# Moving the small constant tiles ahead of the large buffers, with one pad tile, in an encoder kernel

## The chip, the cores and the metric

One core of a Trainium2 chip runs the whole program. The metric is device time in microseconds of that core, from one launch; three runs of the kernel before stand behind its median. The core has five engines that work side by side: TensorE (PE, with its weight loads listed apart as PEld), VectorE (DVE), ScalarE (ACT), GpSimd (POOL) and the one that issues DMAs (SP). On-chip memory has 128 partitions; an address here is a byte offset inside a partition, the same in all of them.

## The reference

A two-layer encoder over 512 tokens of width 1024, all in float32. Each layer adds to `x` four blocks, each of the RMS-normed `x`:

```python
x = x + 0.5 * swiglu(rms_norm(x, ffn1_norm[l]), ffn1_w_in[l], ffn1_w_out[l])
h = rms_norm(x, mix_norm[l])
q, k, v, gu, gv, lx, ly, g = jnp.split(h @ w_mix_in[l], MIX_IN_SPLITS, axis=-1)
...
merged = gates[:, :, 0] * y_attn + gates[:, :, 1] * y_gmlp + gates[:, :, 2] * y_lru
x = x + merged @ w_mix_out[l]
x = x + cross_attention(rms_norm(x, xattn_norm[l]), rms_norm(mem, mem_norm[l]), ...)
x = x + 0.5 * swiglu(rms_norm(x, ffn2_norm[l]), ffn2_w_in[l], ffn2_w_out[l])
```

with `swiglu(h) = (silu(h @ w_in[:, :2816]) * (h @ w_in[:, 2816:])) @ w_out`. A last RMS norm gives the output.

## The kernel before

**Arithmetic.** Every float32 matrix product is made of three matmuls in a reduced float32 type: an operand `a` is split into a high part and the remainder, and `mm3` (L354 to L357) adds high x high, high x low and low x high into one PSUM bank. Written `ps<-a,b` in the profile, `a` is the operand that streams through the array and `b` the one that is loaded into it as weights.

**Buffers.** `x` keeps the residual, transposed, as eight tiles of 128 features by 512 tokens; `xh` and `xl` keep the two parts of `x` times the gain of the next norm, in the same layout (2048 bytes per tile and partition). An arena of 14 slots of 8192 bytes, handed out in quarters of 2048, holds everything else that lives for a while. Weights come from memory in chunks of up to 1 MB into two stage buffers (`stage`, L314), and `split` (L329 to L337) turns parts of up to 1024 columns into `whi` on ACT (L336) and `wlo` on DVE (L337), four buffers of 4096 bytes each, up to four parts ahead of their use.

**Products.** In `pair_unit` (the input half of a feed-forward step: 11 times per half pass, 48 matmuls of 512 columns each) and `gate`, `xh`/`xl` stream under 128x128 weights cut from `whi`/`wlo`. In the output half (`ffn`: 8 feature tiles of 33 matmuls) slots stream under the same kind of weights. In `wide_unit` it is the other way round: `whi`/`wlo` stream, 512 columns at a time, under weights cut from `xh`/`xl`; the projections q, gv and gu are made so, and the k/v projection with 256 columns. The memory keys (`xk`) stream slots of 256 columns under `whi`/`wlo`. Each matmul has a weight load of its own, which PE runs beside the matmul before it. Transposes stream the identity in `cst`; the row sums of the norms (`row_scale`, L393) stream slots under `ones_r`, a matrix of ones.

**Order.** The program is written out in full; each engine runs its instructions in the order in which they are written, with the side work (attention, scans, norms) stepped in by `tick` between the products. SP issues all DMAs.

**Addresses.** Memory is given out in the order of the code, each tile rounded up to 32 bytes, from a base of 1152 bytes that the program reserves. As the kernel is built, in bytes:

| buffer | address | modulo 2048 | modulo 512 |
|---|---|---|---|
| x, xh, xl | 1152, 17536, 33920 | 1152 | 128 |
| cst, ones, ones_r | 50304, 52864, 53376 | 1152, 1664, 128 | 128 |
| slots 0 to 13 | 56000 + 8192 i | 704 | 192 |
| stage (2), whi (4), wlo (4) | 170688, 187072, 203456 and up, whole multiples of 4096 apart | 704 | 192 |

Slices of these that a matmul reads start whole multiples of 512 bytes behind the start of the buffer.

Of the kernel before, what the change touches and what calls it, by code (L numbers as in the profile page):

```python
# [6 lines left out]
F32 = mybir.dt.float32  # L7
F32R = mybir.dt.float32r
# [6 lines left out]
P = 128  # L15
D = 1024
KD = D // P
S = 512
# [30 lines left out]
NPC = _c  # L49
ROW = 4 * HD + 512  # L50
NCONST = 128 + 2 * NTT * HD


LAGS = ((2, 2), (1, 2))


def branch_order():
    """Units of the gated sum: gate tiles by number, up projections by pairs of tiles."""
    o = []
    for br, lag in LAGS:  # L60
        for m in range(KD):
            o.append(("gate", br, m))
            if m % 2 == 1 and m >= lag:
                o.append(("up", br, (m - lag) // 2))
        o += [("up", br, c) for c in range((KD - lag) // 2, KD // 2)]
    o += [("gate", 0, m) for m in range(KD)]
    return o + [("up", 0, c) for c in range(KD // 2)]
# [3 lines left out]


def plan():
    """Weight chunks in the order of use: (key, [columns of each part], maker of the [128, columns] array)."""
    out = []

    def add(key, parts, make):
        out.append((key, parts, make))

    def block(name, l, k0, nk, cols, n):  # L80
        def make(w):
            a = w[name][l][k0 * P:(k0 + nk) * P].reshape(nk, P, -1)
            a = np.stack([a[:, :, c:c + n] for c in cols], axis=2)
            return a.transpose(1, 0, 2, 3).reshape(P, -1)
        return make

    def ffn(l, w_in, w_out):
        for b in range(NB):
            for j in range(b * JB, (b + 1) * JB):
                first = l == 0 and j == 0 and w_in == "ffn1_w_in"  # L90
                add((w_in, l, j), [256, 256, 512, 1024] if first else [1024, 1024], block(w_in, l, 0, KD, (j * P, D_FF + j * P), P))
            for m in range(KD):
                add((w_out, l, b, m), [768, 640], block(w_out, l, b * JB, JB, (m * P,), P))

    def pairs(name, l, c0, n, tag):
        for c in range(n):
            add((tag, l, c), [1024, 1024],
                block(name, l, 0, KD, (c0 + 2 * c * P, c0 + (2 * c + 1) * P), P))

    def wide(name, l, c0, tag):  # L100
        for h in range(2):
            add((tag, l, h), [1024, 1024], block(name, l, 4 * h, 4, (c0,), 512))

    def up2(name, l, c):
        u = [block(name, l, 0, 4, ((2 * c + i) * P,), P) for i in range(2)]
        return lambda w: np.concatenate([u[0](w), u[1](w)], axis=1)

    for l in range(L):
        ffn(l, "ffn1_w_in", "ffn1_w_out")
        pairs("w_mix_in", l, LX0, 2, "lx")  # L110
        add(("kv", l), [1024, 1024], block("w_mix_in", l, 0, KD, (K0,), 256))
        wide("w_mix_in", l, Q0, "q")
        pairs("w_mix_in", l, LY0, 2, "ly")
        wide("w_mix_in", l, GV0, "gv")
        wide("w_mix_in", l, GU0, "gu")
        for kind, br, i in BRANCH_ORDER:
            if kind == "gate":
                add(("gate", l, br, i), [1024], block("w_mix_in", l, 0, KD, (G0 + br * D + i * P,), P))
            else:
                add(("up", l, br, i), [1024], up2(("attn_up", "gmlp_up", "lru_up")[br], l, i))  # L120
        pairs("w_mix_out", l, 0, 4, "mo")
        pairs("xattn_wkv", l, 0, 4, "xk")
        pairs("xattn_wq", l, 0, 2, "xq")
        wide("xattn_wkv", l, D, "xv0")
        pairs("xattn_wq", l, 512, 2, "xq")
        wide("xattn_wkv", l, D + 512, "xv1")
        for g in range(2):
            for c in range(2):
                cols = (4 * g * P + 2 * c * P, 4 * g * P + (2 * c + 1) * P)
                add(("wo", l, g, c), [768, 768], block("xattn_wo", l, 0, 6, cols, P))  # L130
            add(("wo2", l, g), [1024], block("xattn_wo", l, 6, 2, tuple((4 * g + i) * P for i in range(4)), P))
        ffn(l, "ffn2_w_in", "ffn2_w_out")
    return out


def pack(w):
    """Lays the inputs out for the chip; moves elements only."""
    f = {n: np.asarray(a) for n, a in w.items()}
    wts = np.concatenate([np.ascontiguousarray(mk(f)).reshape(-1) for _, _, mk in plan()])
    par = np.zeros((P, L, NPC), np.float32)  # L140
# [59 lines left out]


class Arena:
    """Slots of 8 KiB per partition, of either type, given out in quarters; Tile orders the reuse."""

    def __init__(self, pool, n):
        self.pool = pool
# [18 lines left out]
        return best  # L225

    def has(self, *wanted):
        """Whether regions of these (quarters, type) fit together."""
        used = [list(u) for u in self.used]
        kinds = [t[1] for t in self.tiles]  # L230
        for n, dt in wanted:
            b = self.find(n, dt, used, kinds)
            if b is None:
                return False
            used[b[1]][b[2]:b[2] + n] = [True] * n
            kinds[b[1]] = dt
        return True
# [18 lines left out]
def emit(tc, wts, par, rows, ws_t, bd, xt, memt, const, out):  # L256
    nc = tc.nc
    pe, act, dve, pool, sp = nc.tensor, nc.scalar, nc.vector, nc.gpsimd, nc.sync
    chunks = plan()
# [3 lines left out]
    keep = ctx.enter_context(tc.tile_pool(name="keep", bufs=1))  # L263
# [3 lines left out]
    small = ctx.enter_context(tc.tile_pool(name="small", bufs=2))  # L267
    ps_p = ctx.enter_context(tc.tile_pool(name="ps", bufs=8, space=PSUM))

    x = keep.tile([P, KD, S], F32, name="x")  # L270
    xh = keep.tile([P, KD, S], F32R, name="xh")
    xl = keep.tile([P, KD, S], F32R, name="xl")
    cst = keep.tile([P, NCONST], F32, name="cst")
    ones = keep.tile([P, P], F32, name="ones")
    ones_r = keep.tile([P, P], F32R, name="ones_r")
# [2 lines left out]
    mem_row = keep.tile([P, MEM], F32, name="mem_row")  # L278
    pr = [keep.tile([P, NPC], F32, name=f"par{l}") for l in range(L)]
    lam_c = [keep.tile([P, 8], F32, name=f"lam{l}") for l in range(L)]  # L280
    arena = Arena(keep, NSLOT)
    get = arena.get

# [7 lines left out]
    def bank():  # L291
        return ps_p.tile([P, 512], F32, tag="ps", name="ps")

# [1 line left out]
    class Stream:  # L295
        def __init__(self):
            self.parts = []
# [58 lines left out]
        pe.matmul(ps, lhsT=ah, rhs=bl, start=False, stop=False)  # L356
        pe.matmul(ps, lhsT=al, rhs=bh, start=False, stop=stop)  # L357

# [1 line left out]
    tasks = []  # L360
    mark = {}

# [9 lines left out]
        while tasks:  # L372
            tick()

# [1 line left out]
    def rsqrt_small(v, n, tag):  # L376
        b = small.tile([P, n], I32, tag=tag + "b", name="rsb")
        y = small.tile([P, n], F32, tag=tag + "y", name="rsy")
# [7 lines left out]
        return y  # L386

    def row_scale(row, parts, last=None):
        """1 / sqrt(mean + eps) per token of the squares in parts, alike on all partitions."""
        n = row.shape[-1]  # L390
        ps = bank()[:, 0:n]
        for i, a in enumerate(parts):
            pe.matmul(ps, lhsT=ones_r, rhs=a, start=i == 0, stop=last is None and i == len(parts) - 1)  # L393
        if last is not None:
            pe.matmul(ps, lhsT=ones, rhs=last, start=False, stop=True)
        yr, ar = get(1), get(1)
        y, a = yr.f[:, 0:n], ar.f[:, 0:n]
        act.activation(y, ps, AF.Abs_reciprocal_sqrt, scale=1.0 / D, bias=eps_t)
        dve.scalar_tensor_tensor(a, y, -0.5 / D, y, op0=ALU.mult, op1=ALU.mult)
        dve.scalar_tensor_tensor(a, ps, EPS * D, a, op0=ALU.add, op1=ALU.mult)  # L400
        dve.scalar_tensor_tensor(row, a, 1.5, y, op0=ALU.add, op1=ALU.mult)
        yr.free()
        ar.free()

    class Norm:
        """RMSNorm of x by feature tiles: parts of x * gain now, the row scale when all tiles are in."""

        def __init__(self, gain):
            self.gain = gain
# [30 lines left out]
            return row  # L440

    class FinalNorm(Norm):
        """The last RMSNorm, by halves of the tokens, straight to the output."""

        def tile(self, m):
            if m == 0:
# [70 lines left out]
    xhk = [xh[:, k] for k in range(KD)]  # L517
    xlk = [xl[:, k] for k in range(KD)]

# [1 line left out]
    def ffn(l, w_in, w_out, norm, nxt):  # L521
        s_row = None
        for b in range(NB):
# [40 lines left out]
            for g in gs:  # L564
                g.free()

# [1 line left out]
    def mixer(l, norm, nxt):  # L568
        p_ = pr[l]

# [6 lines left out]
        row, gvn = rowr.f[:, 0:4 * HD], gvr.f  # L577
# [135 lines left out]
            gvr.free()  # L713

        def by_token(r, t):
            """Token tile t of [128, (group, token tile, 128)] as [128, group, 128]."""
            return r.f.rearrange("p (g t d) -> p g t d", g=4, t=NTT)[:, :, t]

        def rope(dst, src, t, nh, a_t, b_t):
            """dst = src * A + swapped(src) * B, [128, nh, 64]."""  # L720
            tmp = get(1)
            n = nh * HD
            s3 = src.rearrange("p (h d) -> p h d", h=nh)
# [9 lines left out]
            tmp.free()  # L733

        def head_scale(raw, nh, name):
            """s / sqrt(mean((s raw)^2) + eps) per token and head, laid out [128, head, token tile]."""
            n = nh * HD
            ssq = small.tile([P, nh, NTT], F32, tag=name + "q", name=name + "q")
            for t in range(NTT):
# [165 lines left out]
        lru_task = lru()  # L905
        next(lru_task)

        # input projections
        for c in range(2):
            ps = pair_unit("lx", l, c, xhk, xlk)  # L910
            if c == 0:
# [3 lines left out]
            for i in range(2):  # L915
                t = get(1)
# [25 lines left out]
        for c in range(2):  # L942
            ps = pair_unit("ly", l, c, xhk, xlk)
            for i in range(2):
                t = get(1)
# [17 lines left out]
        for t in range(NTT):  # L963
            act.activation(by_token(u, t), ps[t].rearrange("p (g d) -> p g d", g=4), AF.Gelu_apprx_tanh,
                           scale=scol[:, t:t + 1])
        tasks.append(gmlp())
        tick(3)

        # gates and branch outputs
        def gate(br, m):  # L970
            ps = bank()
            hi, lo = ws.take(("gate", l, br, m))
# [107 lines left out]
        mem_t["h"] = [h3[:, k] for k in range(KD)]  # L1080
        mem_t["l"] = [l3[:, k] for k in range(KD)]

# [1 line left out]
    def xattn(l, norm, nxt):  # L1084
        drain()
        kt_h, kt_l = getr(4), getr(4)
# [145 lines left out]
            r.free()  # L1232

    def lam_prep(l):
        """-8 softplus(-lam): max(-lam, 0) + 2 atanh(e / (2 + e)), e = exp(-|lam|)."""
        lam = pr[l][:, PC["lam"]:PC["lam"] + 8]
        z = [small.tile([P, 8], F32, tag=f"lz{i}", name=f"lz{i}") for i in range(5)]
        dve.tensor_scalar(z[0], lam, -1.0, None, op0=ALU.mult)
# [72 lines left out]
```

## Time and profile before

| | |
|---|---|
| median of three runs | 2709.33 us (2707.06 to 2711.34) |
| profiled execution | span 2707.8 us, 30194 instructions; no other time of its own is given |
| PE busy | 2666.5 us, 98% |
| PEld / DVE / ACT / POOL busy | 81% / 51% / 43% / 15% |
| DMA | 254.31 MB, 94 GB/s on the mean |

A span runs from the first to the last instruction. A busy share is the time in which an engine has at least one instruction under way; matmuls overlap one another, so the time from one start to the next, not the duration of one, tells the pace. PEclk is the granted clock of TensorE in tenths, of which the full one is 2.4 GHz and the lower level 1.2 GHz.

### The profile page before, as it was taken

What the parts mean: (1) busy time and instruction counts of PE and PEld (TensorE: products, weight loads), DVE (VectorE), ACT (ScalarE), POOL (GpSimd) and SP (SyncE); (2) the same over time, 40 slices, a digit from 0 to 9 for tenths busy, and PEclk for the clock granted to TensorE, in tenths of its full rate; (3) what the DMA queues carried; (4) which work ended last, traced back from release to release, by engine and by line L of the source; (5) the groups of instructions that cost most, each with busy time, mean ns of one, the idle gap of its engine ahead of it and who ended that gap; (6) DMA issues with size and microseconds to landing.
All of it is one profiled execution on the core that took longest, in us unless ns stands there. A gap on an engine that the chain in (4) does not pass through costs nothing.

```text
span 2707.8 us, 30194 instructions
## 1 busy us (share of the span) xinstructions
PE 2666.5 (98%) x12213; PEld 2183.8 (81%) x12213; DVE 1387.2 (51%) x1965; ACT 1161.7 (43%) x1655; POOL 401.1 (15%) x301
## 2 busy tenths in 40 slices
PE   8999999999999999999999999989999999999998
PEld 6888888788878888888888888878888888888886
DVE  5433457766655554334443344577675664533333
ACT  5322336866634442222332223478575343422223
POOL 3101115100121021001111011240000300210111
PEclk9999999999999999999999999999999999999999
DMA  5232231222233222232322322321222232322222
GB/s 178 79 114 94 84 114 71 78 71 78 86 109 109 90 97 97 83 109 84 108 97 74 134 94 75 116 78 62 78 78 94 94 125 78 109 84 95 107 76 74
DMA packets 50123, 254.31 MB, mean 94 GB/s; under 512 B 5440, under 2 KB 11072, under 8 KB 31808
## 3 DMA queue, kind: packets, MB, share of 16 engines
q1 hardware_dynamic: 49984, 252.39, 26.4%
q8 instruction: 95, 1.56, 0.2%
q14 instruction: 44, 0.36, 0.0%
HBM read 250.27 MB, written 2.10 MB: 93 GB/s over the span
## 4 chain that ended last, share of the span: by engine, by line
PE 91%; DVE 4%; ACT 2%; POOL 1%; issue 1%; DMA 0%; SPq 0%; DVEq 0%; POOLq 0%; ACTq 0%
PE ps L356 29%; PE ps L355 29%; PE ps L357 29%; PE ps L858 1%; PE ps L829 1%; PE ps L846 1%; POOL slot L1011 1%; DVE wlo L337 1%; DVE slot L484 1%; DVE slot L1007 0%; ACT slot L483 0%; DMA x<-in_xt 0%; DVE rsy L385 0%; ACT whi L336 0%; POOL nacc L427 0%
## 5 line engine op out<-in xcount | busy, mean ns | idle before, releaser
L336 ACT CAST whi<-stage 128x1024 fp32r<-128x1024 f32 (+2 forms) x506 | 490.9, 971 | 1075.0 <-PE ps L356 939.7
L337 DVE TENSOR_TENSOR wlo<-stage,whi 128x1024 fp32r<-128x1024 f32 (+2 forms) x506 | 588.8, 1164 | 485.6 <-ACT whi L336 483.5
L355 PE MATMUL ps<-xh,whi 128*128 128x512 f32 x2048 | 811.7, 397 | 1.7 <-ACT xh L417 1.7
L356 PE MATMUL ps<-xl,whi 128*128 128x512 f32 x2048 | 808.3, 395 | 0.8 <-DVE xl L418 0.7
L357 PE MATMUL ps<-xh,wlo 128*128 128x512 f32 x2048 | 808.1, 395 | 0.0
L355 PE MATMUL ps<-slot,whi 128*128 128x512 f32 (+1 forms) x1291 | 488.0, 378 | 2.6 <-ACT slot L483 2.6
L356 PE MATMUL ps<-slot,whi 128*128 128x512 f32 (+1 forms) x1291 | 487.0, 377 | 1.1 <-DVE slot L484 1.1
L357 PE MATMUL ps<-slot,wlo 128*128 128x512 f32 (+1 forms) x1291 | 486.4, 377 | 0.0
L355 PEld LDWEIGHTS ps<-xh,whi 128*128 128x128 f32 x2048 | 383.7, 187 | 96.5 <-ACT xh L417 3.3
L356 PEld LDWEIGHTS ps<-xl,whi 128*128 128x128 f32 x2048 | 383.7, 187 | 95.8 <-DVE xl L418 2.4
L357 PEld LDWEIGHTS ps<-xh,wlo 128*128 128x128 f32 x2048 | 383.6, 187 | 93.6
L533 POOL TENSOR_TENSOR slot<-slot,srow 128x512 f32<-128x512 f32 x88 | 148.7, 1689 | 928.6 <-ACT slot L532 928.6
L355 PEld LDWEIGHTS ps<-slot,whi 128*128 128x128 f32 x1291 | 242.9, 188 | 48.8 <-ACT slot L483 3.5
L356 PEld LDWEIGHTS ps<-slot,whi 128*128 128x128 f32 x1291 | 243.0, 188 | 46.8 <-DVE slot L484 2.0
L357 PEld LDWEIGHTS ps<-slot,wlo 128*128 128x128 f32 x1291 | 242.9, 188 | 44.5
L483 ACT CAST slot<-slot 128x512 fp32r<-128x512 f32 (+2 forms) x149 | 89.5, 608 | 280.2 <-DVE slot L534 216.0
L427 POOL TENSOR_TENSOR nacc<-nacc,slot 128x512 f32<-128x512 f32 x62 | 97.2, 1567 | 570.7 <-ACT slot L426 299.5
L531 DVE TENSOR_TENSOR slot<-ps,srow 128x512 f32<-128x512 f32 x88 | 60.8, 691 | 229.1 <-PE ps L357 229.0
L484 DVE TENSOR_TENSOR slot<-slot,slot 128x512 fp32r<-128x512 f32 (+2 forms) x149 | 103.4, 701 | 91.1 <-ACT slot L483 90.8
L534 DVE TENSOR_TENSOR slot<-slot,ps 128x512 f32<-128x512 f32 x88 | 60.5, 687 | 111.7 <-POOL slot L533 111.7
L484 DVE TENSOR_TENSOR slot<-ps,slot 128x512 fp32r<-128x512 f32 (+1 forms) x144 | 92.5, 655 | 40.4 <-ACT slot L483 39.3
L483 ACT CAST slot<-ps 128x512 fp32r<-128x512 f32 (+1 forms) x144 | 77.3, 564 | 58.7 <-PE ps L357 55.4
(192 smaller groups left out, 2268.6 us busy)
## 6 DMA issues: line engine op xcount, KB each, us to landing
stage<-in_wts SPq DMA_DIRECT2D x141, 1024.0 KB, 4.8
stage<-in_wts SPq DMA_DIRECT2D x64, 704.0 KB, 4.0
stage<-in_wts SPq DMA_DIRECT2D x77, 512.0 KB, 3.2
stage<-in_wts SPq DMA_DIRECT2D x8, 768.0 KB, 4.5
slot<-in_memt SPq DMA_DIRECT2D x6, 512.0 KB, 3.3
slot<-in_bd SPq DMA_DIRECT2D x4, 512.0 KB, 5.9
out<-slot SPq DMA_DIRECT2D x8, 256.0 KB, 2.6
x<-in_xt SPq DMA_DIRECT2D x1, 1024.0 KB, 9.2
```

Source lines behind the costliest of these rows:

```text
L336: act.copy(hi[:, 0:n], t)
L337: dve.tensor_tensor(lo[:, 0:n], t, hi[:, 0:n].bitcast(F32), op=ALU.subtract)
L355: pe.matmul(ps, lhsT=ah, rhs=bh, start=start, stop=False)
L356: pe.matmul(ps, lhsT=ah, rhs=bl, start=False, stop=False)
L357: pe.matmul(ps, lhsT=al, rhs=bh, start=False, stop=stop)
L427: pool.tensor_tensor(self.acc, self.acc, sq.f, op=ALU.add)
L483: act.copy(hi, src)
L484: dve.tensor_tensor(lo, src, hi.bitcast(F32), op=ALU.subtract)
L531: dve.tensor_tensor(t.f, psa, s_row, op=ALU.mult)
L533: pool.tensor_tensor(t.f, t.f, s_row, op=ALU.mult)
L534: dve.tensor_tensor(t.f, t.f, psb, op=ALU.mult)
L829: pe.matmul(ps, lhsT=qt[e].r[:, c0:c0 + P], rhs=kk.r[:, k0:k0 + 512], start=part == 0, stop=part == 1)
```

## The change

The three large tiles `x`, `xh` and `xl` are made behind the small ones instead of ahead of them, and a tile of 336 floats (1344 bytes) that nothing reads or writes is put between. The other lines of the diff take comments and docstrings away.

```diff
+PAD = 336
...
-    x = keep.tile([P, KD, S], F32, name="x")
-    xh = keep.tile([P, KD, S], F32R, name="xh")
-    xl = keep.tile([P, KD, S], F32R, name="xl")
     cst = keep.tile([P, NCONST], F32, name="cst")
     ones = keep.tile([P, P], F32, name="ones")
     ones_r = keep.tile([P, P], F32R, name="ones_r")
...
     pr = [keep.tile([P, NPC], F32, name=f"par{l}") for l in range(L)]
     lam_c = [keep.tile([P, 8], F32, name=f"lam{l}") for l in range(L)]
+    keep.tile([P, PAD], F32, name="pad")
+    x = keep.tile([P, KD, S], F32, name="x")
+    xh = keep.tile([P, KD, S], F32R, name="xh")
+    xl = keep.tile([P, KD, S], F32R, name="xl")
     arena = Arena(keep, NSLOT)
```

By the sizes in the code (NCONST is 640, NPC 120) `cst` then starts at 1152, `ones` at 3712, `ones_r` at 4224, the pad at 6848, `x` at 8192, `xh` at 24576, `xl` at 40960, slot 0 at 57344, the stage buffers at 172032, `whi` at 188416 and `wlo` at 204800. From `x` on, all of these are multiples of 2048.

## Rows read from the trace of the kernel before

**Rows 1.** The page: span, then busy us (share) xinstructions, then PEclk by slices.
```profile
span 2707.8 us, 30194 instructions
...
PE 2666.5 (98%) x12213; PEld 2183.8 (81%) x12213; DVE 1387.2 (51%) x1965; ACT 1161.7 (43%) x1655; POOL 401.1 (15%) x301
...
PEclk9999999999999999999999999999999999999999
```

**Rows 2.** The page: the chain that ended last, shares by engine.
```profile
PE 91%; DVE 4%; ACT 2%; POOL 1%; issue 1%; DMA 0%; SPq 0%; DVEq 0%; POOLq 0%; ACTq 0%
```

**Rows 3.** The list of waits, all engines: us in total, times, longest us.
```profile
ACT whi L336 <- PE ps L356: 939.7, 336, 4.8
...
PE ps L800 <- DVE slot L807: 14.3, 3, 8.2
...
ACT whi L336 <- DMA stage<-in_wts: 8.9, 4, 3.7
```

**Rows 4.** Timeline of PE, 1112 to 1296 us: start, duration, line, op; three rows.
```profile
1112.63 0.39 PE L355 MATMUL ps<-slot,whi 128*128 128x512 f32 x1
...
1172.49 0.39 PE L355 MATMUL ps<-xh,whi 128*128 128x512 f32 x1
...
1295.69 0.39 PE L355 MATMUL ps<-slot,whi 128*128 128x512 f32 x1
```

**Rows 5.** The same timeline, 419 to 442 us.
```profile
419.51 0.39 PE L355 MATMUL ps<-whi,xh 128*128 128x512 f32 x1
...
441.49 0.39 PE L355 MATMUL ps<-slot,slot 128*128 128x512 f32 x1
```

**Rows 6.** The same timeline, 408 to 414 us.
```profile
407.81 0.28 PE L357 MATMUL ps<-whi,xl 128*128 128x256 f32 x1
...
413.93 0.28 PE L357 MATMUL ps<-whi,xl 128*128 128x256 f32 x1
```

**Rows 7.** The same timeline, 835 to 841 us.
```profile
834.73 0.28 PE L355 MATMUL ps<-slot,whi 128*128 128x256 f32 x1
...
840.97 0.28 PE L356 MATMUL ps<-slot,whi 128*128 128x256 f32 x1
```

**Rows 8.** Groups by line and form, whole span: xcount | busy us, mean ns | idle before.
```profile
L355 PE MATMUL ps<-xh,whi 128*128 128x512 f32 x2048 | 811.7, 397 | 1.7 <-ACT xh L417 1.7
...
L355 PE MATMUL ps<-slot,whi 128*128 128x512 f32 x1141 | 445.5, 390 | 2.6 <-ACT slot L483 2.6
...
L355 PEld LDWEIGHTS ps<-xh,whi 128*128 128x128 f32 x2048 | 383.7, 187 | 96.5 <-ACT xh L417 3.3 <-ACT slot L964 0.5 <-issue 0.5
...
L483 ACT CAST slot<-slot 128x512 fp32r<-128x512 f32 x128 | 79.2, 621 | 275.1 <-DVE slot L534 216.0 <-POOL slot L1011 44.6 <-DVE slot L872 6.3
...
L355 PE MATMUL ps<-whi,xh 128*128 128x512 f32 x192 | 77.6, 404 | 1.5 <-DVE slot L946 1.5
...
L426 ACT ACTIVATE slot<-x 128x512 f32<-128x512 f32 x62 | 38.0, 618 | 7.1 <-DVE x L560 7.1
...
L846 PEld LDWEIGHTS ps<-cst,slot 128*128 128x128 f32 x256 | 29.9, 140 | 4.3
...
L355 PE MATMUL ps<-whi,xh 128*128 128x256 f32 x64 | 17.8, 279 | 0.0
```

**Rows 9.** Two stretches: us, then PE, PEld, DVE, ACT, POOL busy (x), PEclk, DMA.
```profile
0.00:42.00 42.00, 34.29 (x131) 25.77 (x132) 25.62 (x34) 27.42 (x43) 19.56 (x21) 0.96 0.60 211
445.00:545.00 100.00, 91.17 (x388) 73.42 (x387) 78.92 (x112) 80.80 (x116) 27.23 (x22) 0.93 0.21 74
```

**Rows 10.** Timeline of PE around 1000 us.
```profile
999.93 0.40 PE L357 MATMUL ps<-xh,wlo 128*128 128x512 f32 x1
1000.16 0.63 PE L393 MATMUL ps<-slot,ones_r 128*128 128x512 f32 x2
1000.63 0.39 PE L355 MATMUL ps<-xh,whi 128*128 128x512 f32 x1
```

## The prediction

> **What bounds the kernel.** Read first the page's busy shares [rows 1]: TensorE is busy for 2666.5 of 2707.8 us, so only 41.3 us of the span has no matmul in it, and its clock stands in the top step of the slices nearly throughout. The chain that ended last is PE for 91% [rows 2]. The list of waits [rows 3] shows the rest of the machine waiting for it: ACT's split of the weights stands 939.7 us in all for matmuls to give their buffers back, while PE's own longest entry is 14.3 us. So the time is the sum of the matmul paces, and nothing else needs to be costed in detail. The profiled execution has no time of its own beside its span; the median of the timed runs, 2709.33 us, lies 1.5 us above that span, and I add changes to the median.
>
> Next come the paces, from start to start in the timeline. In the output half of a feed-forward step, from 1112.63 to 1172.49 us, the 8 feature tiles x 33 = 264 matmuls that stream a slot under weights `whi`/`wlo` take 59.86 us: 226.7 ns each. In the input half behind it, to 1295.69 us, 11 x 48 = 528 matmuls that stream `xh`/`xl` under the same weights take 123.20 us: 233.3 ns each [rows 4]. Both are 128x128 by 512 columns at the full clock with no idle time. The only difference in the program is which buffer streams. The wide projections, which stream `whi`/`wlo` under weights from `xh`/`xl`, take 21.98 us for 96, 228.9 ns each [rows 5]. For 256 columns: 54 starts of the k/v projection, weights from `xh`/`xl`, in 6.12 us, 113.3 ns each [rows 6]; 52 starts of the memory keys, weights from `whi`/`wlo`, in 6.24 us, 120.0 ns each [rows 7]. Between 512 and 256 columns of the slot kind lie 106.7 ns, so 256 columns cost 106.7 and 512 cost 213.4. The excess over that is 19.9 ns (xh streams), 13.3 (slot streams), 15.5 (wide), 6.6 (k/v) and 13.3 (memory keys): steps of about 6.65 ns, three, two, some two and a third, one, two.
>
> Put beside the addresses (the section on the kernel lists them): modulo 512 bytes `xh` and `xl` lie at 128, slots, `whi` and `wlo` at 192. Slices lie whole multiples of 512 bytes apart, and in the timeline no slice stands out from its neighbours. (streamed, weights) is (128,192) for 233.3, (192,192) for 226.7, (192,128) for 228.9 and 113.3. The weight load runs beside the streaming, and it is slower there: 187 ns under `xh` against 140 ns beside the short transposes [rows 8]. So two reads of the same memory seem to disturb each other, by an amount that the two offsets set.
>
> **The change, part by part.** The tiles only move. The small tiles in front take 2560+512+512+32+32+1024+480+480+32+32 = 5696 bytes, the pad 1344, and with the base of 1152 `x` starts at 8192; every later buffer moves up by 1344 bytes. All four of `xh`, `xl`, slots and `whi`/`wlo` then lie at 0 modulo 512. No instruction, transfer or wait is added; the pad is never touched. `cst`, `ones` and `ones_r` stay at 128 modulo 512, so not every operand is moved; these serve the transposes and the row sums only.
>
> No row has the pair (0,0), so its price is bounded from both sides. Upwards: the least excess of any row, one step of 6.6 ns, would make 512 columns cost 220.0. Downwards: the largest, 233.3 for everything. The nearest row is (192,192): there, as after the change, both operands start at the same offset. I take its 226.7.
>
> - `xh`/`xl` streamed: 3 x 2048 = 6144 matmuls [rows 8]. I leave out some 350 of them (an estimate: the 131 matmuls of the first 42 us, and the xh part of 388 in 445 to 545 us and of the like stretch of layer two), for there the mean clock is 0.96 and 0.93 and PE waits [rows 9]. 5800 x 6.6 ns = **38.3 us saved**.
> - Wide projections: 3 x 192 = 576 [rows 8] x (228.9 - 226.7) = 1.3 us saved.
> - k/v projection: 3 x 64 = 192 [rows 8] x (120.0 - 113.3) = 1.3 us lost.
> - Slots streamed: 3 x 1141 = 3423 [rows 8], already at this pace: nothing.
> - ACT, DVE and POOL: the ACT rows show no price for the offset (618 ns reading `x` at 128, 621 ns reading a slot at 192 [rows 8]); they lie beside matmuls anyway. Nothing, with 3 ns per instruction as either end.
> - Transfers write to other addresses with the same bytes. ACT waits 8.9 us in all for staged weights [rows 3]: nothing taken, 8.9 us at most to gain; as much to lose if landing got later, since the weight stream runs ahead of PE.
> - What is late next: ACT and DVE feed weights ahead of PE, and a pace 2.8% faster eats a small part of ACT's 939.7 us of standing [rows 3]. The cover stays.
>
> Sum: -38.3 - 1.3 + 1.3 = -38.3 us, 2709.3 - 38.3 = **2671 us**.
>
> What the Trainium skill says speaks against all this: "SBUF — State Buffer", section "Who interferes with whom", gives TensorE two independent read ports and says that it never waits on anyone; by that an offset could cost nothing, and the sum would be 2709. The paces of rows 4 to 7 differ although PE, clock and shape are the same, so the trace does not agree as long as the offsets are the reason.
>
> **Rivals.**
> 1. *Slower: the offset of the streamed operand alone decides*, and 0 modulo 128 (as `xh` has) is the bad one. Then xh streams stay at 233.3, and slots join them: 3423 x 6.6 = 22.6 us, wide 576 x 4.4 = 2.5, k/v 1.3, in all +26.4: **2736 us**. For it: at 999.93 us an `xh` matmul runs while `ones_r`, also at 128, is loaded, and the three matmuls up to 1000.63 take 0.70 us, 233 ns each [rows 10], where equal offsets at 226.7 would have given 0.68 for the three; there are five such places. Against it: with the streamed offset the same, the weights' offset changes 120.0 to 113.3. It decides as soon as the slot matmuls of the output halves leave 226.7 upwards while those of the input halves do not fall.
> 2. *Nothing: the offset is not the reason*, and the paces of `xh` and slots differ by another cause, such as who writes them or how far they lie from the weights. **2709 us**. For it: ACT does not see the offset [rows 8], and a trace names buffers, not addresses. Against it: the 264 matmuls [rows 4] stream eleven regions of slots, which are scattered over 112 KiB, at one pace. (This is also what the skill's section above would give.)
> 3. *More: aligned rows lose a further step*, and one of 6.6 ns is left. 5800 x 13.3 = 77 us, 3423 x 6.7 = 23, wide 576 x 8.9 = 5: -105, **2604 us**. For it: k/v has such an excess; against: only with 256 columns.
>
> **How the numbers follow.** Forecast 0.46, rival 1 0.26, rival 2 0.13, rival 3 0.15. The forecast has the nearest row; rival 1 has the five places that contradict equal offsets, though they are single matmuls between others. Within 0.2% (5.4 us, about what a measurement of this kernel can tell from no change) lies rival 2 alone: faster 0.61, same 0.13, slower 0.26. The forecast's own range is 2660 to 2682 (the transfers' 8.9 us and some of the 350 matmuls). Since rivals of both signs hold 0.41, the range goes from 2604 (rival 3) to 2737 (rival 1), and leaves out a larger gain than 105 us and a loss above 28.
>
> **What would show it.** In the changed kernel's timeline the starts of an input half: 528 x 226.7 = 119.7 us instead of 123.2; an output half unchanged at 59.9; k/v at 120. The busy PE time falls by 38 us and the idle 41 us stays. An input half still at 123.2 with an output half near 61.6 is rival 1; both unchanged is rival 2; both below 118 and 59 is rival 3. The forecast is wrong if the pace of (0,0) is not that of (192,192), whatever the total does.

## The result, and the profile after

The changed kernel takes 2672.17 us (median of four runs, 2668.25 to 2675.11) where the kernel before, in four runs beside it, takes 2709.44: a ratio of 0.9859, 95% interval 0.9847 to 0.9871. That is 37.3 us less. The forecast was 2671.

Each line number of the profile after is two higher than before (`mm3` is L357 to L359, `whi` L338). The page of the changed kernel, the lines that answer to [rows 1, 2]:

```profile
span 2671.8 us, 30194 instructions
...
PE 2627.4 (98%) x12213; PEld 2189.5 (82%) x12213; DVE 1391.8 (52%) x1965; ACT 1161.6 (43%) x1655; POOL 400.6 (15%) x301
...
PE 91%; DVE 4%; ACT 2%; POOL 1%; issue 1%; DMA 0%; SPq 0%; DVEq 0%; POOLq 0%; ACTq 0%
```

The instructions are as many as before, the chain is the same, and DVE, ACT and POOL are busy within 5 us of what they were. PE's busy time alone falls, by 39.1 us; its idle time goes from 41.3 to 44.4, and the span from 2707.8 to 2671.8. ACT's wait for PE in the list of waits of the changed kernel, the answer to [rows 3]:

```profile
ACT whi L338 <- PE ps L358: 904.2, 331, 4.6
```

It stands 35.5 us less than before, as an engine does that waits for a faster one. So the whole gain is the pace of the matmuls. The timeline of PE in the changed kernel shows which ones (start, duration, line, operation): the same output half and input half as in [rows 4], then the wide projection of [rows 5] and 54 starts of the k/v projection, [rows 6].

```profile
1097.72 0.39 PE L357 MATMUL ps<-slot,whi 128*128 128x512 f32 x1
...
1157.57 0.39 PE L357 MATMUL ps<-xh,whi 128*128 128x512 f32 x1
...
1277.24 0.39 PE L357 MATMUL ps<-slot,whi 128*128 128x512 f32 x1
...
413.36 0.39 PE L357 MATMUL ps<-whi,xh 128*128 128x512 f32 x1
...
435.12 0.39 PE L357 MATMUL ps<-slot,slot 128*128 128x512 f32 x1
...
400.05 0.28 PE L359 MATMUL ps<-whi,xl 128*128 128x256 f32 x1
...
406.53 0.28 PE L359 MATMUL ps<-whi,xl 128*128 128x256 f32 x1
```

The output half takes 59.85 us for 264 starts, 226.7 ns each, as before. The input half takes 119.67 us for 528, 226.6 ns where it was 233.3. The wide projection takes 21.76 us for 96, 226.7 ns where it was 228.9. The k/v projection takes 6.48 us for 54, 120.0 ns where it was 113.3: that one is slower. Added up over all starts of the two timelines, the `xh`/`xl` streams fall by 37.8 us (1448.2 to 1410.4 for 6144 of them), the wide ones by 1.4, slots by 0.3, and k/v rises by 1.2.

### The profile page after: what moved, and what is told of

The parts are those of the page before. It is cut to its first block, busy times and chain, and to the rows that moved or that the text cites. A ratio compares the mean times of both kernels' runs of the same rounds, so it can differ in the third digit from the quotient of the medians.

```text
span 2671.8 us, 30194 instructions
## 1 busy us (share of the span) xinstructions
PE 2627.4 (98%) x12213; PEld 2189.5 (82%) x12213; DVE 1391.8 (52%) x1965; ACT 1161.6 (43%) x1655; POOL 400.6 (15%) x301
## 4 chain that ended last, share of the span: by engine, by line
PE 91%; DVE 4%; ACT 2%; POOL 1%; issue 1%; DMA 0%; SPq 0%; DVEq 0%; POOLq 0%; ACTq 0%
PE ps L357 29%; PE ps L358 29%; PE ps L359 29%; PE ps L860 1%; PE ps L831 1%; PE ps L848 1%; POOL slot L1013 1%; DVE wlo L339 1%; DVE slot L486 1%; DVE slot L1009 0%; ACT slot L485 0%; DMA x<-in_xt 0%; DVE rsy L387 0%; POOL nacc L429 0%; ACT whi L338 0%
## 5 line engine op out<-in xcount | busy, mean ns | idle before, releaser
L338 ACT CAST whi<-stage 128x1024 fp32r<-128x1024 f32 (+2 forms) x506 | 491.7, 973 | 1036.6 <-PE ps L358 904.2
L357 PE MATMUL ps<-xh,whi 128*128 128x512 f32 x2048 | 802.7, 392 | 1.5 <-ACT xh L419 1.3
L358 PE MATMUL ps<-xl,whi 128*128 128x512 f32 x2048 | 799.4, 390 | 1.9 <-DVE xl L420 1.9
L359 PE MATMUL ps<-xh,wlo 128*128 128x512 f32 x2048 | 798.7, 390 | 0.0
L357 PE MATMUL ps<-slot,whi 128*128 128x512 f32 (+1 forms) x1291 | 488.5, 378 | 2.6 <-ACT slot L485 2.6
L359 PE MATMUL ps<-slot,wlo 128*128 128x512 f32 (+1 forms) x1291 | 486.9, 377 | 0.0
L357 PEld LDWEIGHTS ps<-xh,whi 128*128 128x128 f32 x2048 | 385.1, 188 | 82.4 <-ACT xh L419 3.0
L359 PEld LDWEIGHTS ps<-xh,wlo 128*128 128x128 f32 x2048 | 385.0, 188 | 79.9
L357 PEld LDWEIGHTS ps<-slot,whi 128*128 128x128 f32 x1291 | 243.0, 188 | 48.1 <-ACT slot L485 3.5
L359 PEld LDWEIGHTS ps<-slot,wlo 128*128 128x128 f32 x1291 | 242.9, 188 | 44.4
```

The costliest lines, as they stand in the source:

```text
L338: act.copy(hi[:, 0:n], t)
L357: pe.matmul(ps, lhsT=ah, rhs=bh, start=start, stop=False)
```

## The experiments

The question left by the result is what about the addresses counts. Three theories stood against each other. **R**: the *difference* between the offset of the weights and that of the streamed operand, wherever the two lie. **S**: the offset of the streamed operand alone (the first rival; before, `xh` lay at 128). **A**: that operands lie on multiples of 512 bytes, as the change has it.

Most experiments move buffers by a few bytes with unused tiles; w_plus16, w_plus4 and k256_plus64 start operands later inside their buffers, and wlo_apart gives one kind of buffer a pool of its own. Each runs as many instructions as the kernel before, 30194. For most of them, the fence behind it shows the same two stretches: an output half (264 starts, slots stream under `whi`/`wlo`) and the input half behind it (528 starts, `xh`/`xl` stream), from a table by windows. Its columns are the window, its length in us, then busy us and instructions of PE, PEld, DVE, ACT and POOL, the granted clock, the DMA share and GB/s. The windows begin and end on starts in the timeline, so the length divided by 264 or 528 is the pace. The clock is 1.00, the 2.4 GHz level, in all of them.

**Equal offsets without the change's order.** The kernel before with one unused tile of 448 bytes ahead of the arena: the constants stay where they were, and `x`, slots and weights all lie at 128 modulo 512, none on a multiple of 512.

```
+    keep.tile([P, 112], F32, name="pad")
     arena = Arena(keep, NSLOT)
```

> The order of tiles before is kept (x first, at 1152) and one pad of 448 bytes stands between the small tiles and the slots, so x, slots and weights all lie at 128 modulo 512. Theory R (what counts is the weights' offset less the streamed operand's): equal offsets, so the paces of the change: input half of a feed-forward step 528 starts in 119.7 us, output half 264 starts in 59.9 us, k/v 120 ns per start, total 2672 us. Theory S (the streamed operand's own offset counts, and 128 is the bad one): 233.3 ns for all, input half 123.2, output half 61.6, total 2736 us. Theory A (a start on a multiple of 512 counts): nothing lies on one, so nothing gained, total 2709 us.

```profile
1096.60:1156.44 59.84, 59.84 (x265) 49.55 (x264) 21.08 (x26) 14.46 (x19) 1.39 (x1) 1.00 0.33 113
1156.44:1276.12 119.68, 119.68 (x530) 99.10 (x528) 47.91 (x54) 33.88 (x42) 17.56 (x10) 1.00 0.25 89
```

2671.34 us (four runs, 2670.12 to 2672.68), ratio 0.9859, interval 0.9842 to 0.9875: the whole gain of the change, with both halves at 226.7 ns. S and A fall. The order of the constants and the multiples of 512 and 2048 play no part.

**Equal offsets with no pad at all.** The changed kernel with its `pad` tile taken out; the buffers then lie at 192 modulo 512, and use not a byte more than before.

```
-    keep.tile([P, PAD], F32, name="pad")
```

> The constants in front, no pad tile at all: every large buffer then lies at 192 modulo 512, none on a multiple of 256. Theory R (only the difference between the streamed operand's offset and the weights' counts, modulo 256 bytes): 512 columns at 227 ns throughout, 2672 us, as the changed kernel. Rival (the place itself has some part, 0 and 128 being good places): xh streams above 227 and a time between 2672 and 2709 us.

2671.35 us (four runs, 2671.21 to 2672.35), ratio 0.9856, interval 0.9843 to 0.987, and the same paces (59.84 and 119.68 us). The place has no part of its own: 0, 128 and 192 give one time.

**Differences one by one.** Three kernels give `x`, slots and weights three different offsets, by the size of the `pad` and two more unused tiles (the sizes here are those of the first of them):

```
-PAD = 336
+PAD = 80
...
+    keep.tile([P, 32], F32, name="pad_b")
+    pad_p.tile([P, 112], F32, name="pad_c")
     arena = Arena(keep, NSLOT)
```

> The changed kernel with x, xh, xl at 0, slots at 128, whi and wlo at 64 modulo 512. Theory R: xh streams meet weights 64 bytes ahead, as in the kernel before: input half 123.2 us; slots meet weights 64 behind, as the wide projections before: output half 264 x 228.9 ns = 60.4 us; wide and k/v stay at 228.9 and 113.3 ns; total about 2717 us. Theory S: input half 119.7 us (streams at 0), output half 61.6 us (streams at 128), total about 2695 us. Theory A: the streamed xh on its multiple of 512 keeps 119.7 us, slots lose.

```profile
1114.94:1175.37 60.43, 60.43 (x266) 49.62 (x264) 21.06 (x26) 14.42 (x19) 1.40 (x1) 1.00 0.32 112
1175.37:1298.56 123.19, 123.19 (x530) 99.47 (x529) 47.95 (x54) 33.85 (x42) 17.62 (x10) 1.00 0.25 86
```

2716.99 us. `xh` and `xl` lie at 0 modulo 512, as in the changed kernel, and their streams are back at 233.3 ns with the weights 64 bytes off. Slots, 64 off on the other side, take 228.9.

> x, xh, xl at 0, slots at 64, whi and wlo at 128 modulo 512. Theory R: slots now meet weights 64 ahead: output half 264 x 233.3 ns = 61.6 us; for xh the difference is 128, which no row has: between 220.0 and 233.3 ns per start, input half 116.2 to 123.2 us. Theory S: input half 119.7 us whatever the weights do. Theory A: as S.

```profile
1119.80:1181.39 61.59, 61.59 (x266) 49.74 (x264) 21.06 (x26) 14.43 (x19) 1.41 (x1) 1.00 0.31 110
1181.39:1304.08 122.69, 122.69 (x529) 99.56 (x528) 47.94 (x54) 33.82 (x42) 17.63 (x10) 1.00 0.25 87
```

2729.69 us: 128 apart costs 232.4 ns in this input half (the 480 starts from 1007.80 us of the same run stand at 233.3), 64 apart 233.3, now with slots as the streamed side.

> x, xh, xl at 0, slots at 224, whi and wlo at 256 modulo 512. Theory R with a period of 256 bytes: xh against weights counts as equal, input half 119.7 us; with a period of 512 it is a new pair, between 116.2 and 123.2 us. Slots meet weights 32 bytes ahead, half of a step of 64: between 59.9 us (as equal) and 61.6 us (as 64 ahead) for the output half. Theory S: input half 119.7 us; nothing said of streams at 224.

```profile
1102.90:1164.50 61.60, 61.60 (x266) 49.66 (x264) 21.07 (x26) 14.43 (x19) 1.39 (x1) 1.00 0.32 110
1164.50:1284.20 119.70, 119.70 (x529) 99.13 (x528) 47.92 (x54) 33.81 (x42) 17.58 (x10) 1.00 0.25 89
```

2692.75 us. 256 apart is as good as equal, 226.7 ns, so the period is 256 bytes and not 512; 32 apart costs the whole step, 233.3.

> x, xh, xl at 0, slots at 448, weights at 96 modulo 512: differences 96 for the xh streams and 160 (that is -96 modulo 256) for slots, two places not measured yet. Theory R with equal offsets as the best place: both between 228.5 and 233.3 ns, so between 2672 + 6072 x 1.5 + 3429 x 1.5 = 2687 us and 2672 + 6072 x 6.5 + 3429 x 6.5 = 2734 us. Rival (equal offsets are only a good place, and a better one lies between): a pace below 226.7 in one of the two, and with both below it a time under 2672 us.

```profile
1122.62:1184.23 61.61, 61.61 (x265) 49.56 (x264) 21.05 (x26) 14.44 (x19) 1.40 (x1) 1.00 0.33 110
1184.23:1307.92 123.69, 123.69 (x529) 99.44 (x528) 47.95 (x54) 33.82 (x42) 17.57 (x10) 1.00 0.25 86
```

2739.61 us, above the top of what was expected: 96 apart gives 234.3 ns, the slowest input half of all runs, and 96 on the other side 233.4. No better place than equal has turned up.

**How exact must it be?** Every `whi` and `wlo` starts 16 bytes, then 4 bytes (one element), later in its buffer; the buffers are made 256 bytes longer for it. For 16 bytes, on top of all_at_192 (the cast and the subtraction then write `hi` and `lo` as they are; for 4 bytes `o` is 1):

```
-            hi = w_p.tile([P, HALF], F32R, tag="hi", name="whi")
-            lo = w_p.tile([P, HALF], F32R, tag="lo", name="wlo")
+            hi = w_p.tile([P, HALF + 64], F32R, tag="hi", name="whi")
+            lo = w_p.tile([P, HALF + 64], F32R, tag="lo", name="wlo")
+            o = 4
+            hi, lo = hi[:, o:o + n], lo[:, o:o + n]
```

> As all_at_192, with every whi and wlo starting 16 bytes later in its buffer (buffers 256 bytes longer): difference 16 for all streams. If operands are read in pieces of 32 bytes or more, so that 16 is no other place: 227 ns and 2671 us (256 columns at 120). Rival (any difference costs the whole step, as 32 did with 232.8 ns): 6072 x 5.8 + 3429 x 6.5 = 57.5 us more, 2729 us. In between (a cost that grows with the difference): about 2700 us.

```profile
1117.22:1178.82 61.60, 61.60 (x265) 49.88 (x264) 21.06 (x26) 14.43 (x19) 1.40 (x1) 1.00 0.32 110
1178.82:1302.02 123.20, 123.20 (x529) 99.77 (x528) 47.91 (x54) 33.79 (x42) 17.63 (x10) 1.00 0.24 86
```

> As w_plus16 with one element, 4 bytes. Pieces of 32 bytes: 2671 us, as w_plus16. Any difference costs the whole step: 2729 us. A cost that grows with the difference: a quarter of what w_plus16 shows above 2671.

```profile
1116.25:1177.60 61.35, 61.35 (x265) 49.55 (x264) 21.09 (x26) 14.46 (x19) 1.40 (x1) 1.00 0.32 111
1177.60:1300.30 122.70, 122.70 (x530) 99.10 (x529) 47.98 (x54) 33.83 (x42) 17.64 (x10) 1.00 0.24 87
```

2727.61 and 2724.61 us: 233.3 ns in both halves at 16 bytes, 232.4 at 4. One element off loses 5.7 of the 6.6 ns in these halves. The expectation of coarse pieces fell, and so did the one of a cost that grows with the difference. The other way round it costs more: in the wide projections of w_plus4 the streamed `whi`/`wlo` are the ones that lie 4 bytes later, and 96 starts take 22.78 us, 237.3 ns each, the slowest of all runs among the wide projections that have no waits in them.

```profile
421.95:444.73 22.78, 22.78 (x97) 18.17 (x96) 15.66 (x30) 16.53 (x25) 10.32 (x12) 1.00 0.26 93
```

The whole step at 16 bytes does not hold throughout, however. In the middle of layer one of w_plus16 the timeline of PE reads:

```profile
954.45 0.39 PE L357 MATMUL ps<-slot,whi 128*128 128x512 f32 x1
...
993.89 0.39 PE L357 MATMUL ps<-xh,whi 128*128 128x512 f32 x1
...
1004.77 0.62 PE L395 MATMUL ps<-slot,ones_r 128*128 128x512 f32 x2
1005.22 0.39 PE L357 MATMUL ps<-xh,whi 128*128 128x512 f32 x1
...
1117.22 0.39 PE L357 MATMUL ps<-slot,whi 128*128 128x512 f32 x1
```

The 174 starts that stream slots take 39.44 us and the 48 of `xh`/`xl` behind them 10.88, 226.7 ns each: the pace of equal offsets, with weights 16 bytes off. After the two row sums the next 480 starts of `xh`/`xl`, at the same offsets, take 112.00 us, 233.3 each. Layer two does the same (from 2302.31 us). So at unequal offsets the difference alone does not settle the pace; what else does is open. At 4 bytes no such stretch was found, and with equal offsets no slow one: every stretch of 90 or more `xh` or slot starts lies between 226.7 and 227.2 ns there (starts over 260 ns left out).

**One odd buffer.** First `xl` alone is moved, to 224 modulo 256, 32 bytes from the weights. The other two matmuls of each `mm3` stream `xh`, at 0, under weights at 256. Then, from all_at_192, `wlo` alone is moved by 32 bytes, with a pool of its own.

```
+    keep.tile([P, 56], F32, name="pad_l")
     xl = keep.tile([P, KD, S], F32R, name="xl")
+    keep.tile([P, 8], F32, name="pad_m")
```

> Layout of the change with xl alone moved to 224 modulo 256 (slots and weights at 256, xh at 0 modulo 512). If each single matmul pays for its own pair: the third of the input half that streams xl goes to 232.8 ns, the two thirds that stream xh stay at 227; 2024 x 5.8 ns = 11.7 us and about 1 us for wide matmuls under xl: 2685 us. Rival (a neighbour in the sequence pays too, since the weight load of one matmul runs beside the streaming of another): all three at 229 to 233 ns, 2690 to 2709 us.

```profile
1107.94:1167.78 59.84, 59.84 (x266) 49.57 (x264) 21.07 (x26) 14.46 (x19) 1.40 (x1) 1.00 0.33 113
1167.78:1289.80 122.02, 122.02 (x529) 99.31 (x528) 47.94 (x54) 33.84 (x42) 17.59 (x10) 1.00 0.25 87
```

2699.43 us, where a price for each pair by itself would have given 2685. The input half is at 231.1 ns on the mean: (231.1 - 226.7) / 6.6 is two thirds of the step, though only a third of the pairs is unequal. By role, the means over these 528 starts are 228.0 ns for `xh` ahead of `xl`, 233.3 for `xl`, 232.0 for the `xh` behind it. So a neighbour pays too, above all the one behind. (The first 377 input starts of this run, from 27.41 us, stand at 233.3 on the mean, again with the same offsets.)

```
+    pad_p = ctx.enter_context(tc.tile_pool(name="pad_p", bufs=1))
+    wl_p = ctx.enter_context(tc.tile_pool(name="wl", bufs=NW))
...
+    pad_p.tile([P, 8], F32, name="pad_w")
...
-            lo = w_p.tile([P, HALF], F32R, tag="lo", name="wlo")
+            lo = wl_p.tile([P, HALF], F32R, tag="lo", name="wlo")
```

> As all_at_192 with wlo alone 32 bytes later, at 224: now the weights change place from one matmul to the next and the streamed operands don't. Theory 1 (a stream pays for the weight load that runs beside it, and for nothing else): of three matmuls only the second, which streams while wlo is loaded for the third, goes to 232.8 ns; (2024 + 1143) x 5.8 ns = 18 us, 2690 us. Theory 2 (neighbours pay too, as in xl_apart, there 4.7 ns on the mean of three): 9500 x 4.7 = 45 us, 2716 us. Theory 3 (in xl_apart it was the change of place between streamed operands that cost): nothing, 2671 us.

```profile
1116.79:1178.39 61.60, 61.60 (x266) 49.53 (x265) 21.03 (x26) 14.45 (x19) 1.40 (x1) 1.00 0.32 110
1178.39:1301.59 123.20, 123.20 (x530) 99.06 (x529) 47.92 (x54) 33.88 (x42) 17.55 (x10) 1.00 0.25 86
```

2728.85 us, above all three expectations. Both halves stand at 233.3 ns on the mean, the whole step, with the weights of one matmul in three out of place. The matmuls do not share it evenly, as the timeline of PE shows:

```profile
1201.49 0.40 PE L358 MATMUL ps<-xh,whi 128*128 128x512 f32 x1
1201.72 0.40 PE L359 MATMUL ps<-xl,whi 128*128 128x512 f32 x1
1201.96 0.39 PE L360 MATMUL ps<-xh,wlo 128*128 128x512 f32 x1
1202.19 0.40 PE L358 MATMUL ps<-xh,whi 128*128 128x512 f32 x1
```

Over the 528 starts of this input half the means are 232.0 ns for the first of the three, 239.1 for the second, which streams while `wlo` is loaded for the third, and 228.9 for the third. Theory 1 named the slowest matmul, but gave it 232.8 and nothing to the others: that a stream pays only for the weight load beside it falls a second time. How much a mixed set costs is not a sum over its pairs; what it is made of stays open.

**256 columns.** On top of all_at_192, the weights of the k/v projection and of the memory keys alone start 64 bytes later in their buffers, since w128_slots64 had shown 113.4 ns for the memory keys at such a difference, where equal offsets give 120.

```
+            o = 16 if chunks[i][0][0] in ("kv", "xk") else 0
+            hi, lo = hi[:, o:o + n], lo[:, o:o + n]
```

> As all_at_192, but the high and low weights of the k/v projection and of the memory keys start 64 bytes later in their buffer (buffers 256 bytes longer, so that all others stay equal modulo 256). Theory R with a table of its own for 256 columns: 441 matmuls of the memory keys fall from 119.7 to about 113.4 ns as in w128_slots64 (2.7 us), 190 of k/v from 119.9 to between 113.3 and 117.8 (1.2 to 0.4 us): 2668 to 2669 us. Rival (these stretches are bound by something else than the pace): the pace falls and the time stays at 2672 us.

The table by windows of all_at_192 for 95 starts of the memory keys and 96 of the k/v projection, then the same two of k256_plus64:

```profile
820.77:832.16 11.39, 11.39 (x97) 11.39 (x96) 7.83 (x10) 5.90 (x9) 0.00 (x0) 1.00 0.46 156
396.45:408.04 11.59, 11.59 (x99) 11.59 (x98) 6.10 (x16) 4.96 (x13) 3.51 (x9) 1.00 0.28 93
```

```profile
821.23:832.01 10.78, 10.78 (x97) 10.77 (x95) 7.78 (x10) 5.88 (x9) 0.00 (x0) 1.00 0.45 150
399.05:410.44 11.39, 11.39 (x100) 11.39 (x98) 6.06 (x16) 4.97 (x13) 3.51 (x9) 1.00 0.29 94
```

These are starts of layer one. The same 95 starts of the memory keys in layer two of k256_plus64:

```profile
2138.87:2150.06 11.19, 11.19 (x97) 11.19 (x95) 7.83 (x10) 5.89 (x9) 0.00 (x0) 1.00 0.46 156
```

2668.12 us (five runs, 2666.87 to 2668.93), ratio 0.9843, interval 0.983 to 0.9857. Its runs lie below all four of all_at_192, measured beside it, by 3.2 us in the medians. The memory keys go from 119.9 to 113.5 ns over these starts of layer one, as expected, but in layer two only to 117.8, with the same offsets; k/v goes only from 120.7 to 118.6, though the same difference had given 114.2 over the same 96 starts before (113.3 in the 54 of [rows 6]). In the two profiled executions the memory keys gain 1.4 us in all, where 2.7 were expected, and k/v 0.4, so the total met its forecast in part by luck: the other 1.3 of the 3.1 us by which the spans differ are not traced to the change. (Of the 441 starts in the expectation, 59 are the last output half in 256 columns, whose weights did not move.) This is the fastest version measured. Against the changed kernel, 2672.17, it gains 4 us by a comparison of separate runs.

## Why the prediction was right

- *PE's pace is the time* [rows 1 to 3]: right. Busy PE time fell by 39.1 us and the span by 36.0. The idle time did not stay at 41.3, as expected, but rose to 44.4.
- *The price of equal offsets is that of the nearest row*, (192,192) at 226.7 ns [rows 4]: right, and shown rather than argued by all_at_128 and all_at_192. This step carried the number.
- *38.3 us on `xh`/`xl`*: measured 37.8. *1.3 on the wide ones*: 1.4. *1.3 lost on k/v*: 1.2. *Slots nothing*: 0.3. The net term of 38.3 stands against 37.3 in the medians.
- *The weight load is slower beside the stream (187 against 140 ns), so two reads disturb each other* [rows 8]: this ground does not carry. In the kernel before, the loads under slots, whose offsets were equal, last 188 ns as well, and the loads under `xh` still last 188 after the change. The forecast did not need it, since its price came from the row (192,192). The row of the page before:

```profile
L355 PEld LDWEIGHTS ps<-slot,whi 128*128 128x128 f32 x1291 | 242.9, 188 | 48.8 <-ACT slot L483 3.5
```

- *ACT, DVE, POOL and the transfers nothing*: right; the casts of `whi` still lie beside matmuls and ACT still waits 904.2 us for PE.
- *Rival 1, the streamed offset alone.* Fell in all_at_128, and in w64_slots128 from the other side. What had spoken for it, the row-sum matmuls [rows 10], was misread: there `xh` and `ones_r` were both at 128, but the matmuls around them had weights and slots at 192. In all_at_128 everything there lies at 128, and the timeline of PE reads:

```profile
987.12 0.39 PE L358 MATMUL ps<-xh,wlo 128*128 128x512 f32 x1
987.35 0.62 PE L394 MATMUL ps<-slot,ones_r 128*128 128x512 f32 x2
987.80 0.39 PE L356 MATMUL ps<-xh,whi 128*128 128x512 f32 x1
```

  Three matmuls take 0.68 us where they took 0.70: the pace of equal offsets. Three starts among unequal neighbours could not price a pair, as xl_apart and wlo_apart show.
- *Rival 2, the offset is not the reason.* Fell: in w64_slots128 `xh` has the same address modulo 512, the same writer and the same instructions as in the changed kernel, and streams at 233.3. So the rule of the Trainium skill weighed there ("SBUF — State Buffer", section "Who interferes with whom": TensorE's two read ports are independent), taken to mean that an offset can cost nothing, does not hold for this kernel's pace: 226.7 against 233.3 ns with nothing but the offsets moved.
- *Rival 3, a further step on aligned rows.* Not seen. Its ground was a base of 213.4 ns, twice the 106.7 between 512 and 256 columns at (192,192). That difference was taken between a good row (226.7) and a bad one (120.0). Of the paces measured for 256 columns the best is 113.3, and twice that is about 226.7, the pace of equal offsets at 512. No stretch of `xh` or slot streams in any run is faster; that this is a floor is not shown beyond that.

## What to carry to other kernels

When a matmul stream is bound by its own pace, compare the paces of like matmuls that differ only in their buffers, and put the buffers' byte offsets beside them: here the best pace held throughout only where all operands of a stream started at the same offset modulo 256 bytes. One element off lost most of the step, and one odd kind of buffer cost two thirds of it (`xl`) or, on the mean, all of it (`wlo`). Whole multiples of 512 or 2048 bought nothing beyond that. For 256 columns the best place was another one, so measure each shape.

## What the runs showed that was not expected

- The period is 256 bytes (w256_slots224), and one element is enough to lose most of the step (w_plus4: 232.4 ns). Yet at unequal offsets the same operands can run at two paces (w_plus16: 226.7 and 233.3 ns).
- 512 and 256 columns want opposite things: equal offsets give 226.7 ns at 512 columns, the best seen, and 120 at 256, where 64 bytes apart gives 113.4 for the memory keys in the best stretches. Both steps are 6.6 ns per matmul. Here too the difference alone does not settle the pace: the memory keys of k256_plus64 differ between the layers (113.4 and 117.8), and so does k/v between kernels (over those 96 starts 114.2 ns before, 118.6 in w64_slots128 and 118.6 in k256_plus64, all with `xh` 64 bytes below `whi`); why is open.
- The weight loads are no shorter with equal offsets: the loads under `xh` last 188 ns on the mean, 187 before [rows 8], while the matmuls beside them are 6.6 ns apart. That two reads collide in the memory is an inference from the offsets; no row shows the collision itself. A row of the changed kernel's groups by form:

```profile
L357 PEld LDWEIGHTS ps<-xh,whi 128*128 128x128 f32 x2048 | 385.1, 188 | 82.4 <-ACT xh L419 3.0 <-issue 0.7 <-DVE nb L837 0.5
```
